# Two gated feed-forward layers: where the norm's factor 1/rms is applied

## The chip, the cores and the metric

The kernel runs on one core of a Trainium2 chip. The metric is the device time of one execution in microseconds, as the median of several runs. The engines are TensorE (PE, with PEld for its weight loads), VectorE (DVE), ScalarE (ACT), GpSimd (POOL) and SyncE (SP), which here only issues DMAs.

## The reference, cut to what matters

256 tokens of width 1024 pass through four layers of a first block (mixer, then feed-forward, each followed by a layer norm) and one layer of a second block: a gated feed-forward layer, a mixer, a second gated feed-forward layer, a last norm. The change concerns the two gated layers:

```python
def rmsnorm(x, g):
    y = x * rsqrt(mean(x * x, -1) + 1e-6)      # one factor for each token
    return y * g                               # one weight for each column

def swiglu(x, w1, w3, w2):                     # w1, w3: 1024 x 2816, w2: 2816 x 1024
    return (silu(x @ w1) * (x @ w3)) @ w2

x = x + 0.5 * swiglu(rmsnorm(x, ffn1_norm), ffn1_w1, ffn1_w3, ffn1_w2)
x = x + hybrid_mixer(rmsnorm(x, mix_norm), ...)
x = x + 0.5 * swiglu(rmsnorm(x, ffn2_norm), ffn2_w1, ffn2_w3, ffn2_w2)
```

Since the factor is the same for all columns of a token, `rmsnorm(x) @ w1` is `((x * g) @ w1)` with each token's sums multiplied by its factor.

## The kernel before, in words

**Weights.** All weights come from memory once, in a fixed order (`STREAM`), in items of up to 128x1024 floats. Each is cast on ScalarE to the rounded four-byte form that TensorE takes at full rate (line 366, the high part), and VectorE subtracts to get the rest (line 367, the low part; most are issued at line 369). Products are three matmuls: high by high, high by low, low by high. `get` (line 408) hands out the next item and first calls `pump`, which issues DMAs up to 8 items ahead and casts and low parts up to 5 items ahead, as far as 6 raw and 7 split buffers allow. The instructions of each engine run in the order in which the code issues them; nothing reorders them.

**Postponed steps.** `then(f, ...)` puts a step on a list, and the next `get` runs the list (`flush`) behind its `pump`. So each step of a chain that is put off in this way lies one weight later than the step before it.

**Rows and boundaries.** Token rows lie in two tiles of 128 tokens, x[0] and x[1]. `boundary` (line 1679) interleaves the end of one layer with the start of the next: the last products of the layer before (`down_tail`), then for each row tile the residual with its norm (`fin`), eight transposes (`to_xT`, line 613, into xT in two halves of 512 columns) and their copies, and between them the first matmuls of the next layer. `ln_rms` and `rms` give the `fin` of the two gated layers; both end in `rms_rows` (line 660): two squares on ScalarE with a sum, one small sum and one scale on VectorE, a power on GpSimd, and two products of 128x512 on VectorE, which multiply the row by the factor and by the weight.

**The front.** `front` (line 525) starts a layer with six weights, numbered 0 to 5 here, in an order that needs the first 128 tokens first. It yields to `boundary` at two stops for the transposes of x[1], then goes through weights 0 to 5 once more with what is left: per weight the last 4 matmuls with the high part and 8 with the low part, then a step of `low_next` (one postponed low part; all postponed ones at weight 3, lines 549 and 550), `flush`, `done` and `pump`. `done` sums the two halves of the weight's bank on VectorE (`front_sum`, line 559).

**The gated layer.** `ffn` (line 1310) has 22 hidden tiles of 128 columns (numbered from 0). The front's six weights are w1 and w3 of tiles 0 to 2; the following weights, numbered on from 6, are w1 and w3 of tile 3, and so on. A tile's two sums (128x256 each) lie in one tile `su`. Behind the second sum, `evac` is put off by a weight: tanh of half the first sum on ScalarE; one weight later `evac_on`: two VectorE steps, (tanh + 1) * a and the product with b, and the cast of the result on ScalarE (line 1327); one weight later the subtraction for its low part. From tile 5 on each tile also has a w2 weight, whose product (`down`, 12 matmuls of 512 columns) takes the hidden tile of five tiles before; the last four hidden tiles go through `down_tail`.

Of the kernel before, what the change touches and what calls it, by code (L numbers as in the profile page):

```python
# [9 lines left out]
F32 = mybir.dt.float32  # L10
F32R = mybir.dt.float32r
I32 = mybir.dt.int32
AF = mybir.ActivationFunctionType
# [5 lines left out]
P = 128  # L19
S = 256  # L20
D = 1024
# [3 lines left out]
RMS_EPS = 1e-6  # L25
# [254 lines left out]
def kernel(ctx, tc, d, out, dbg=None):  # L280
    nc = tc.nc
    ctx.enter_context(tc.manual_schedule())
    nv, ns, ng, nt = nc.vector, nc.scalar, nc.gpsimd, nc.tensor
# [7 lines left out]
    sm = ctx.enter_context(tc.tile_pool(name="sm", bufs=4))  # L291
    accp = ctx.enter_context(tc.tile_pool(name="accp", bufs=1, space=PSUM))
# [4 lines left out]
    def stt(o, a, s, b, op0, op1):  # L297
        nv.scalar_tensor_tensor(out=o, in0=a, scalar=s, in1=b, op0=op0, op1=op1)  # L298

    def tt(o, a, b, op, eng=None):  # L300
        (eng or nv).tensor_tensor(out=o, in0=a, in1=b, op=op)  # L301

    def ts2(o, a, s1, s2, op0, op1):
        nv.tensor_scalar(out=o, in0=a, scalar1=s1, scalar2=s2, op0=op0, op1=op1)  # L304

    def ts1(o, a, s1, op0):
        nv.tensor_scalar(out=o, in0=a, scalar1=s1, scalar2=None, op0=op0)

    def act(o, i, f, **kw):
        ns.activation(out=o, in_=i, func=f, **kw)  # L310

    def mm(o, a, b, start, stop):
        nt.matmul(out=o, lhsT=a, rhs=b, start=start, stop=stop)  # L313

    MUL, ADD, SUB, MAX = ALU.mult, ALU.add, ALU.subtract, ALU.max

    def psb(name="pp"):
        return pp.tile([P, 512], F32, tag="pp", name=name)
# [56 lines left out]
    def then(f, *a):  # L375

        st["then"].append((f, a))
# [30 lines left out]
    def get(name):  # L408
        i = st["i"]
        e = STREAM[i]  # L410
        assert e[1] == name, (i, e, name)
        if not st["pin"]:
            st["base"] = i
        pump(i + 1)
        flush()
        st["i"] += 1
        hl = st["hl"].pop(i)
        if i in WHOLE:
            return hl
        c, kk = _width(e), e[4]  # L420
        return [hl[:, n, :c].rearrange("p (k w) -> p k w", k=kk) for n in range(2)]
# [11 lines left out]
    def ws2(bank, ch, xT, kk, c0=0):  # L433


        h, l = ch
        w = slice(c0, c0 + P)
        for k in range(kk):
            mm(bank, h[:, k, w], xT[:, k], k == 0, False)
            mm(bank[:, :S], l[:, k, w], xT[:, k, 0, :], False, k == kk - 1)  # L440

    def ws2_sum(bank, o):
        nv.tensor_reduce(out=o, in_=bank.rearrange("p (a n) -> p n a", a=2), axis=AX.X, op=ADD)  # L443
# [43 lines left out]
    def acc_new():  # L487
        return [[accp.tile([P, 512], F32, tag=f"a{t}{n}", name=f"a{t}{n}") for n in range(2)]
                for t in range(2)]
# [69 lines left out]
    def front_sum(ps, o):  # L559

        nv.tensor_reduce(out=o.rearrange("p (t n) -> p t n", t=2),
                         in_=ps.rearrange("p (t a n) -> p t n a", t=2, a=2), axis=AX.X, op=ADD)

    def front_banks():

        n = [0]

        def bank():
            n[0] += 1
            if n[0] > 2:  # L570
                return psb("fr")
            tag = f"a0{n[0] - 1}"
            return accp.tile([P, 512], F32, tag=tag, name=tag)
        return bank


    def new_x(t):
        return xp.tile([P, D], F32, tag=f"x{t}", name=f"x{t}")
# [7 lines left out]
    def C(k, a=0, n=None):  # L586
        part, o, w = COFF[k]
        return cs[part][:, o + a:o + (w if n is None else a + n)]

    x = [new_x(t) for t in range(2)]  # L590
# [10 lines left out]
    ident = C("ident")  # L601
# [3 lines left out]
    def rsqrt(o, v, mul, add):  # L605

        n = v.shape[-1]
        e = sm.tile([P, 16], F32, tag="ve", name="ve")
        ts2(e[:, :n], v, mul, add, MUL, ADD)
        tt(o, e[:, :n], mhalf[:, :n], ALU.pow, ng)  # L610
# [22 lines left out]
    halves = [slice(0, 512), slice(512, 1024)]  # L633
# [18 lines left out]
    def residual(x, acc_t, t, c):  # L652
# [4 lines left out]
                yield  # L657
        return z

    def rms_rows(x, g, t):  # L660
        o = new_x(t)
        ss = sm.tile([P, 2], F32, tag="ss", name="ss")
        for n, w in enumerate(halves):
            act(o[:, w], x[:, w], AF.Square, accum_out=ss[:, n:n + 1])
        tt(ss[:, 0:1], ss[:, 0:1], ss[:, 1:2], ADD)
        rs = sm.tile([P, 1], F32, tag="rs", name="rs")
        rsqrt(rs, ss[:, 0:1], 1.0 / D, RMS_EPS)
        for w in halves:
            stt(o[:, w], x[:, w], rs, g[:, w], MUL, MUL)
        return o  # L670
# [636 lines left out]
            yield from down_tail(acc, lambda c: (oT[:, 4 + c], get("mla_w_o")), 4)  # L1307
            fes.close()

    def ffn(seg, xT):  # L1310
        nf = DFF2 // P
        lag = FFN_LAG
        w = [f"ffn{seg}_w{k}_2" for k in (1, 3, 2)]
        tail = TAIL["ffn", seg]
        with tc.tile_pool(name="ffnp", bufs=8) as mp:
            hid = {}

            def evac(j, a, b):
                r = mp.tile([P, S], F32, tag="r", name="r", bufs=2)
                act(r, a, AF.Tanh, scale=0.5)  # L1320
                then(evac_on, j, r, a, b)

            def evac_on(j, r, a, b):
                h = mp.tile([P, 2, S], F32R, tag="h", name="h")
                stt(r, r, 1.0, a, ADD, MUL)
                tt(r, r, b, MUL)
                ns.copy(out=h[:, 0], in_=r)  # L1327
                then(tt, h[:, 1], r, h[:, 0].bitcast(F32), SUB)
                hid[j] = h

            sums = {}

            def done(n, ps):
                if n % 2 == 0:
                    sums[0] = mp.tile([P, 2, S], F32, tag="su", name="su", bufs=3)
                front_sum(ps, sums[0][:, n % 2])
                if n % 2 == 1:
                    then(evac, n // 2, sums[0][:, 0], sums[0][:, 1])

            yield from front([w[k % 2] for k in range(FRONT)], xT, front_banks(), done,  # L1340
                             (4, 5) if seg == 1 else (3, 4))
            acc = acc_new()
            for j in range(FRONT // 2, nf + lag):
                if j < nf:
                    su = mp.tile([P, 2, S], F32, tag="su", name="su", bufs=3)
                    for n in range(2):
                        ps = psb()
                        ws2(ps, get(w[n]), xT, KD)
                        ws2_sum(ps, su[:, n])
                    then(evac, j, su[:, 0], su[:, 1])  # L1350
                c = j - lag
                if c < 0:
                    continue
                if c < nf - tail:
                    ch = get(w[2])
                    for t in range(2):
                        down(acc, t, hid[c], ch, c == 0, False)
            yield from down_tail(acc, lambda j: (hid[nf - tail + j], get(w[2])), tail)
# [320 lines left out]
    def boundary(prev, fin, nxt):  # L1679


        def rest(f):
            while True:
                try:
                    next(f)
                except StopIteration as e:
                    return e.value

        f = fin(0, next(prev))
        next(f)  # L1690
        low_next(1)
        y0 = rest(f)
        xT = new_xT()
        f = fin(1, next(prev))
        next(f)
        to_xT(xT, y0, 0, (0,))
        next(prev)
        to_xT(xT, y0, 0, (1,))
        next(prev)
        next(prev, None)  # L1700
        g = nxt(xT)
        next(g)
        y1 = rest(f)
        to_xT(xT, y1, 1, (0,))
        next(g)
        to_xT(xT, y1, 1, (1,))
        return g
# [6 lines left out]
            return x[t]  # L1714
        return fin

    def ln_rms(i, n, name):
        last = ln(i, n)
        g = rows(name, (0,), tabp, "gC")

        def fin(t, a):
            return rms_rows((yield from last(t, a)), g, t)
        return fin

    def rms(name, c):
        g = rows(name, (0,), gbp, "gB")

        def fin(t, a):
            x[t] = yield from residual(x[t], a, t, c)
            return rms_rows(x[t], g, t)  # L1730
        return fin

    order = [lambda xT: ret(0, xT), lambda xT: mlp(0, xT, hook=early), lru, lambda xT: mlp(1, xT), mla,
# [9 lines left out]
    g = order[0](xT0)  # L1743
    for i in range(7):
        g = boundary(g, ln(i // 2, i % 2), order[i + 1])
# [5 lines left out]
    for t in range(2):  # L1751
        x[t] = new_x(t)
        nc.gpsimd.dma_start(out=x[t], in_=xd[t:S:2, :])
    g = boundary(g, ln_rms(3, 1, "ffn1_norm_2"), lambda xT: ffn(1, xT))
    tap("f3")
    tabs.close()
    g = boundary(g, rms("mix_norm_2", 0.25), lambda xT: mix(xT, bd))
    tap("ffn1")
    g = boundary(g, rms("ffn2_norm_2", 0.5), lambda xT: ffn(2, xT))
    tap("mix")  # L1760
    gf = rows("final_norm_2", (), gbp, "gB")

    for t in range(2):
        a = next(g)
        y = new_x(t)
        ss = sm.tile([P, 2], F32, tag="ss", name="ss")
# [8 lines left out]
        rs = sm.tile([P, 1], F32, tag="rs", name="rs")  # L1775
# [60 lines left out]
```

## Time and profile before

| what | value |
|---|---|
| median of 3 runs | 2014.78 us (2012.68 to 2014.83) |
| the profiled execution's own time | 2014.34 us |
| its span, first to last instruction | 2012.6 us |
| TensorE matmul busy | 1979.8 us, 98% |
| VectorE busy | 1425.1 us, 71% |
| ScalarE busy | 1019.0 us, 51% |
| mean granted clock of TensorE | 0.998 of full speed |

The profile is one execution on the chip. Times in it count from the span's first instruction. In the timeline a row gives the start, the time covered, the engine, the line of the code, the operation, the output and inputs, the shape and the number of merged instructions; in brackets stands the idle time of that engine just ahead of the row and what ended it. The ends of matmuls are modelled, and matmuls are pipelined. The granted clock is given as a share of 2.4 GHz; 0.5 is the level of 1.2 GHz.

### The profile page before, as it was taken

Reading aid. Unit: us, or ns where it says so; the run is one execution under the profiler, and the core shown is the slowest. Engines: PE = TensorE matmul, PEld = TensorE weight load, DVE = VectorE, ACT = ScalarE, POOL = GpSimd, SP = SyncE. Lnnn points to the kernel's source line nnn. Section 1 sums busy time; section 2 is a strip of 40 time slices with the busy share of each in tenths; the row PEclk is TensorE's granted clock in tenths of the full one; section 3 lists DMA queues with packets and bytes.
Section 4 is the critical chain, followed back from the end, with each engine's and each line's share of the span. In section 5 each row is a group of like instructions: output and inputs, shape, how many; then the busy total and the mean of one; then the engine's idle time right before and its main releaser. Section 6 shows DMA issues by size and latency. Waiting matters only on the chain.

```text
span 2012.6 us, 28871 instructions
## 1 busy us (share of the span) xinstructions
PE 1979.8 (98%) x11118; PEld 1708.3 (85%) x11118; DVE 1425.1 (71%) x2057; ACT 1019.0 (51%) x1451; POOL 79.4 (4%) x114
## 2 busy tenths in 40 slices
PE   8999999999999999999999999999999999999998
PEld 6888887887888888888888888888888999998886
DVE  6767876689856688656877875568777755567775
ACT  5444555477555465554444455535444655544443
POOL 0000000000000100000000000000001100000000
PEclk9999999999999999999999999999999999999999
DMA  8654565464755455664655485637655556465652
GB/s 300 183 174 145 192 204 173 145 215 147 238 188 187 135 169 177 201 193 152 220 177 169 136 292 183 195 120 225 190 188 173 154 159 163 137 200 176 210 188 72
DMA packets 102713, 364.53 MB, mean 181 GB/s; under 512 B 11856, under 2 KB 12528, under 8 KB 102577
## 3 DMA queue, kind: packets, MB, share of 16 engines
q1 hardware_dynamic: 97200, 345.09, 53.7%
q0 software_dynamic: 5376, 17.61, 3.5%
q8 instruction: 87, 1.43, 0.3%
q14 instruction: 50, 0.40, 0.1%
HBM read 360.52 MB, written 2.13 MB: 180 GB/s over the span
## 4 chain that ended last, share of the span: by engine, by line
PE 90%; DVE 5%; DMA 1%; ACT 1%; issue 1%; POOL 1%; SPq 0%; POOLq 0%; DVEq 0%; ACTq 0%
PE pp L313 53%; PE a L313 32%; PE fr L313 3%; DVE x L298 1%; DVE hl L301 1%; POOL rs L301 1%; ACT hl L366 1%; DVE bs L640 1%; PE a L621 0%; DMA raw<-in_w_ret_dram 0%; DMA raw<-in_w_mlp_dram 0%; DVE xT L301 0%; PE ao L313 0%; PE a L1578 0%; DMA raw<-in_w_mla_dram 0%
## 5 line engine op out<-in xcount | busy, mean ns | idle before, releaser
L301 DVE TENSOR_TENSOR hl<-raw,hl 128x1024 fp32r<-128x1024 f32 (+3 forms) x659 | 774.5, 1198 | 217.6 <-ACT hl L366 215.7
L366 ACT CAST hl<-raw 128x1024 fp32r<-128x1024 f32 (+3 forms) x659 | 661.8, 1032 | 343.9 <-PE a L313 169.8
L313 PE MATMUL pp<-xT,hl 128*128 128x512 f32 (+1 forms) x4688 | 784.2, 324 | 0.6 <-ACT hl L366 0.3
L313 PEld LDWEIGHTS pp<-xT,hl 128*128 128x128 f32 x4688 | 685.8, 189 | 86.7 <-issue 3.1
L313 PE MATMUL a<-hl,h 128*128 128x512 f32 x2064 | 502.1, 394 | 0.0
L313 PEld LDWEIGHTS a<-hl,h 128*128 128x128 f32 x2064 | 381.4, 190 | 80.9
L313 PE MATMUL pp<-hl,xT 128*128 128x512 f32 (+2 forms) x1200 | 270.8, 381 | 2.7 <-ACT hl L366 1.6
L313 PEld LDWEIGHTS pp<-hl,xT 128*128 128x128 f32 x1200 | 219.6, 189 | 41.5 <-DVE xT L301 2.0
L443 DVE TENSOR_REDUCE su<-pp 128x256 f32<-128x512 f32 x180 | 124.0, 689 | 165.1 <-PE pp L313 161.6
L310 ACT ACTIVATE su<-su 128x512 f32<-128x512 f32 x128 | 81.0, 633 | 132.0 <-DVE su L443 122.2
L301 POOL TENSOR_TENSOR rs<-ve,mhalf 128x1 f32<-128x1 f32 (+2 forms) x48 | 41.9, 875 | 1682.5 <-DVE ve L304 1682.5
L313 PE MATMUL a<-hl,yT 128*128 128x512 f32 x432 | 104.0, 397 | 0.0
L313 PEld LDWEIGHTS a<-hl,yT 128*128 128x128 f32 x432 | 80.7, 188 | 18.8 <-issue 0.5
L313 PE MATMUL fr<-xT,hl 128*128 128x256 f32 x672 | 88.7, 285 | 0.0
L313 PEld LDWEIGHTS fr<-xT,hl 128*128 128x128 f32 x672 | 83.8, 193 | 0.0
L1327 ACT CAST h<-r 128x256 fp32r<-128x256 f32 x44 | 17.9, 407 | 127.1 <-DVE r L301 127.1
L313 PE MATMUL a<-xT,hl 128*128 128x256 f32 x336 | 46.6, 289 | 3.9 <-DVE xT L301 3.9
L313 PEld LDWEIGHTS a<-xT,hl 128*128 128x128 f32 x336 | 42.9, 195 | 7.5 <-DVE xT L301 7.5
L298 DVE SCALAR_TENSOR_TENSOR x<-x,a 128x512 f32<-128x512 f32 x32 | 21.8, 683 | 32.9 <-PE a L313 32.9
L301 DVE TENSOR_TENSOR h<-su,h 128x512 fp32r<-128x512 f32 x64 | 43.8, 685 | 0.9 <-ACT h L785 0.9
L785 ACT CAST h<-su 128x512 fp32r<-128x512 f32 x64 | 39.7, 620 | 2.0
L322 ACT CAST xT<-a 128x512 fp32r<-128x512 f32 x22 | 12.8, 586 | 42.6 <-PE a L621 42.6
(356 smaller groups left out, 1343.7 us busy)
## 6 DMA issues: line engine op xcount, KB each, us to landing
raw<-in_w_mlp_dram SPq DMA_DIRECT2D x256, 512.0 KB, 4.0
raw<-in_w_ffn_dram SPq DMA_DIRECT2D x132, 512.0 KB, 4.1
raw<-in_w_ret_dram SPq DMA_DIRECT2D x128, 512.0 KB, 4.4
raw<-in_w_mix_dram SPq DMA_DIRECT2D x68, 512.0 KB, 4.2
raw<-in_w_lru_dram SPq DMA_DIRECT2D x30, 512.0 KB, 4.6
raw<-in_w_mla_dram SPq DMA_DIRECT2D x12, 512.0 KB, 4.5
raw<-in_w_mix_dram SPq DMA_DIRECT2D x16, 384.0 KB, 4.3
gB<-in_ln_g_dram POOLq DMA_DIRECT2D x8, 512.0 KB, 4.5
```

The source lines that it names most:

```text
L298: nv.scalar_tensor_tensor(out=o, in0=a, scalar=s, in1=b, op0=op0, op1=op1)
L301: (eng or nv).tensor_tensor(out=o, in0=a, in1=b, op=op)
L310: ns.activation(out=o, in_=i, func=f, **kw)
L313: nt.matmul(out=o, lhsT=a, rhs=b, start=start, stop=stop)
L322: ns.copy(out=h, in_=src)
L366: ns.copy(out=hl[:, 0, :c], in_=t[:, :c])
L443: nv.tensor_reduce(out=o, in_=bank.rearrange("p (a n) -> p n a", a=2), axis=AX.X, op=ADD)
L640: nv.bn_stats(out=bs[:, n], in_=z[:, w])
L785: ns.copy(out=h[:, :, 0], in_=r)
L1327: ns.copy(out=h[:, 0], in_=r)
```

## The change

For the two gated layers, `rms_rows` is replaced by `gain_rows`: the row tile is multiplied by the norm's weight alone and goes on to the transposes. The squares, the sum and the power for the factor are issued later, in `done` of the front's weight 0. At `done` of weight 4, `factors` builds two diagonal matrices with the factors of the 256 tokens, multiplies a matrix of ones by them on TensorE, so that every partition holds the factor of each token along its columns, and copies the result to `fac`. Each hidden tile's pair of sums is multiplied by `fac` (one VectorE product of 128x512) ahead of its tanh. The first two tiles' `evac` are put on the list at weight 4 and the third's at weight 5 (before: at weights 1, 3 and 5). The mixer between the two layers keeps `rms_rows`.

```diff
+    def gain_rows(x, g, t, rms):
+
+        o = new_x(t)
+        for w in halves:
+            tt(o[:, w], x[:, w], g[:, w], MUL)
+        rms[t] = sm.tile([P, 1], F32, tag="rs", name="rms")
+
+        def factor():
+            sq = accp.tile([P, 512], F32, tag="a11", name="sq")
+            ss = sm.tile([P, 2], F32, tag="ss", name="ss")
+            for n, w in enumerate(halves):
+                act(sq, x[:, w], AF.Square, accum_out=ss[:, n:n + 1])
+            tt(ss[:, 0:1], ss[:, 0:1], ss[:, 1:2], ADD)
+            rsqrt(rms[t], ss[:, 0:1], 1.0 / D, RMS_EPS)
+        rms[t, "f"] = factor
+        return o
...
-    def ffn(seg, xT):
+    def ffn(seg, xT, rms):
...
-            def evac(j, a, b):
-                r = mp.tile([P, S], F32, tag="r", name="r", bufs=2)
+            fac = mp.tile([P, S], F32, name="fac", bufs=1)
+
+            def factors():
+
+                one = mp.tile([P, P], F32, name="one", bufs=1)
+                nv.memset(one, 1.0)
+                ps = psb()
+                for t in range(2):
+                    dg = mp.tile([P, P], F32, name=f"dg{t}", bufs=1)
+                    ts1(dg, ident, rms[t], MUL)
+                    mm(ps[:, t * P:(t + 1) * P], one, dg, True, True)
+                ns.copy(out=fac, in_=ps[:, :S])
+
+            def evac(j, su):
+                tt(su, su, fac[:, None, :].to_broadcast([P, 2, S]), MUL)
+                a, b = su[:, 0], su[:, 1]
+                r = mp.tile([P, S], F32, tag="r", name="r", bufs=4)
                 act(r, a, AF.Tanh, scale=0.5)
                 then(evac_on, j, r, a, b)
...
             def done(n, ps):
                 if n % 2 == 0:
-                    sums[0] = mp.tile([P, 2, S], F32, tag="su", name="su", bufs=3)
-                front_sum(ps, sums[0][:, n % 2])
-                if n % 2 == 1:
-                    then(evac, n // 2, sums[0][:, 0], sums[0][:, 1])
+                    sums[n // 2] = mp.tile([P, 2, S], F32, tag="su", name="su", bufs=3)
+                front_sum(ps, sums[n // 2][:, n % 2])
+                if n == 0:
+                    for t in range(2):
+                        rms[t, "f"]()
+                elif n == 4:
+                    factors()
+                    for j in range(2):
+                        then(evac, j, sums[j])
+                elif n == 5:
+                    then(evac, 2, sums[2])
...
-                    then(evac, j, su[:, 0], su[:, 1])
+                    then(evac, j, su)
...
-            return rms_rows((yield from last(t, a)), g, t)
+            return gain_rows((yield from last(t, a)), g, t, rms)
...
-            return rms_rows(x[t], g, t)
+            return rms_rows(x[t], g, t) if later is None else gain_rows(x[t], g, t, later)
```

## Rows read from the trace of the kernel before

**Rows 1.** The page, busy time and share of the span by engine.
```profile
PE 1979.8 (98%) x11118; PEld 1708.3 (85%) x11118; DVE 1425.1 (71%) x2057; ACT 1019.0 (51%) x1451; POOL 79.4 (4%) x114
```

**Rows 2.** Timeline of the boundary into the first gated layer.
```profile
1331.49 0.63 PE L621 MATMUL trp<-cs,x 128*128 128x128 f32 x4 [1.02 <-DVE x L298]
...
1334.52 1.22 PE L313 MATMUL a<-xT,hl 128*128 128x256 f32 x8 [0.55 <-DVE xT L301]
...
1339.37 0.75 DVE L298 SCALAR_TENSOR_TENSOR x<-x,rs,bB 128x512 f32<-128x512 f32 x1
1340.15 0.63 ACT L310 ACTIVATE x<-x 128x512 f32<-128x512 f32 x1 [0.73 <-DVE x L298]
...
1342.79 0.66 PE L621 MATMUL a<-cs,x 128*128 128x128 f32 x4 [2.73 <-DVE x L298]
...
1344.84 2.07 PE L313 MATMUL a<-xT,hl 128*128 128x256 f32 x8 [0.34 <-DVE xT L301]
```

**Rows 3.** Windows after that wait: busy time by engine, granted clock, DMA.
```profile
1344.00:1346.00 2.00, 1.66 (x9) 1.28 (x8) 1.54 (x3) 0.65 (x2) 0.00 (x0) 0.52 0.43 145
1346.00:1348.00 2.00, 2.00 (x13) 2.00 (x12) 2.00 (x2) 0.00 (x0) 0.00 (x0) 0.63 0.04 2
```

**Rows 4.** Timeline of the boundary into the second gated layer, TensorE.
```profile
1822.22 0.60 PE L621 MATMUL a<-cs,x 128*128 128x128 f32 x4
...
1824.22 1.22 PE L313 MATMUL a<-xT,hl 128*128 128x256 f32 x8
```

**Rows 5.** Timeline of the fronts, first layer (one row), then second layer.
```profile
1354.69 4.62 DVE L301 TENSOR_TENSOR hl<-raw,hl 128x1024 fp32r<-128x1024 f32 x4
...
1828.84 0.69 DVE L561 TENSOR_REDUCE su<-a 128x256 f32<-128x512 f32 x1 [0.35 <-PE a L313]
1828.88 1.05 ACT L366 CAST hl<-raw 128x1024 fp32r<-128x1024 f32 x1 [4.53 <-PE a L313]
1829.45 1.22 DVE L301 TENSOR_TENSOR hl<-raw,hl 128x1024 fp32r<-128x1024 f32 x1
...
1830.08 5.92 PE L313 MATMUL fr<-xT,hl 128*128 128x256 f32 x48
...
1832.92 3.48 DVE L301 TENSOR_TENSOR hl<-raw,hl 128x1024 fp32r<-128x1024 f32 x3
```

**Rows 6.** Timeline of one tile of the first gated layer, VectorE and ScalarE.
```profile
1392.48 0.68 DVE L443 TENSOR_REDUCE su<-pp 128x256 f32<-128x512 f32 x1
1392.60 0.41 ACT L1327 CAST h<-r 128x256 fp32r<-128x256 f32 x1 [3.08 <-DVE r L301]
...
1393.98 1.23 DVE L301 TENSOR_TENSOR hl<-raw,hl 128x1024 fp32r<-128x1024 f32 x1 [0.82 <-ACT hl L366]
...
1395.13 0.42 DVE L301 TENSOR_TENSOR h<-r,h 128x256 fp32r<-128x256 f32 x1
...
1396.06 2.35 DVE L301 TENSOR_TENSOR hl<-raw,hl 128x1024 fp32r<-128x1024 f32 x2
1398.33 0.41 DVE L298 SCALAR_TENSOR_TENSOR r<-r,su 128x256 f32<-128x256 f32 x1
...
1399.12 0.68 DVE L443 TENSOR_REDUCE su<-pp 128x256 f32<-128x512 f32 x1
```

**Rows 7.** Window over nine tiles of the first gated layer, later on.
```profile
1408.73:1484.51 75.78, 75.78 (x400) 64.64 (x399) 53.08 (x74) 34.07 (x46) 0.00 (x0) 1.00 0.61 189
```

**Rows 8.** Groups by line and shape, VectorE: count, busy us, mean ns.
```profile
L301 DVE TENSOR_TENSOR q<-ra,cosr 128x512 f32<-128x512 f32 x8 | 5.5, 683 | 0.0
...
L304 DVE TENSOR_SCALAR ve<-mv 128x1 f32<-128x1 f32 x32 | 4.9, 154 | 1.1
...
L307 DVE TENSOR_SCALAR pe<-pe,sums 128x256 f32<-128x256 f32 x16 | 4.9, 350 | 0.3
```

**Rows 9.** Timeline, TensorE behind the last hidden weight of each layer.
```profile
1509.33 15.50 PE L313 MATMUL a<-hl,h 128*128 128x512 f32 x66
...
1986.94 16.89 PE L313 MATMUL a<-hl,h 128*128 128x512 f32 x72
```

More of the change, by code (lines that the diff above doesn't have):

```diff
@@ L1715, in ln, with ln_gain @@
         return fin
-    def ln_rms(i, n, name):
+    def ln_gain(i, n, name, rms):
         last = ln(i, n)
@@ L1721, in fin, with rms @@
         def fin(t, a):
-            return rms_rows((yield from last(t, a)), g, t)
+            return gain_rows((yield from last(t, a)), g, t, rms)
         return fin
-    def rms(name, c):
+    def rms(name, c, later=None):
         g = rows(name, (0,), gbp, "gB")
@@ L1753 @@
         nc.gpsimd.dma_start(out=x[t], in_=xd[t:S:2, :])
-    g = boundary(g, ln_rms(3, 1, "ffn1_norm_2"), lambda xT: ffn(1, xT))
+    later = {}
+    g = boundary(g, ln_gain(3, 1, "ffn1_norm_2", later), lambda xT: ffn(1, xT, later))
     tap("f3")
@@ L1758 @@
     tap("ffn1")
-    g = boundary(g, rms("ffn2_norm_2", 0.5), lambda xT: ffn(2, xT))
+    later2 = {}
+    g = boundary(g, rms("ffn2_norm_2", 0.5, later2), lambda xT: ffn(2, xT, later2))
     tap("mix")
```

## The prediction

> **What bounds the kernel now.** I read the page first: TensorE is busy 98% of the span [rows 1], so only two kinds of stretch can move the time, those where TensorE stands still and those where its clock is low. The timeline of the two places where a gated layer begins comes next, since the change takes work off the chain there. At the first layer (from 1330 us) TensorE waits for the second half of the normed rows: the last residual row block is ready at 1339.37 + 0.75 = 1340.12, the squares, the sum, the power on GpSimd and the product follow, and the transposes start at 1342.79 after 2.73 us of idle time; the first half had cost 1.02 and 0.55 us [rows 2]. The windows right after show the granted clock at 0.52 and 0.63, so a part of them ran at the 1.2 GHz level [rows 3]. At the second layer there is no such wait: transposes at 1822.22 and matmuls at 1824.22 follow without a stop [rows 4]. So the norm's chain is worth something at one of the two layers only.
>
> The stretch behind that, the front of six weights, I read on VectorE. It is behind TensorE there: in the second layer TensorE ends the front at 1830.08 + 5.92 = 1836.0, and VectorE only then ends three low parts of later weights (1832.92 + 3.48); in the first layer it is four (4.62 us) [rows 5]. Then I read how VectorE gets out of that backlog [rows 6], and its share once it is out [rows 7].
>
> **What goes.** At the first layer the transposes of the second half need only the gain product of its first 512 columns, 0.69 us after 1340.12, where they now come 2.67 us after it: 1.94 us. The first half gains between 0 and the 1.57 us of its two waits; four casts of weights stand ahead of its transpose copies on ScalarE, which the two squares no longer hold up, but which wait for buffers that TensorE frees, so I take 0.8. The front's second part, at 1344.84 now, starts at 1342.1. The clock, after a wait of some 0.8 us instead of 2.73, should stay up. That is worth more than 0.85 (the first eight matmuls take 2.07 here and 1.22 in the second layer [rows 2, 4]) and less than (1 - 0.52) x 1.66 + (1 - 0.63) x 2.00 = 1.54, the busy time of the two windows that the clock took [rows 3]; I take 1.15. The scaled products of before (0.70) become plain products (0.69): nothing. At the second layer I take 0.
>
> **What is moved.** Four squares (0.63 each [rows 2]) go to ScalarE behind the first front weight. ScalarE is idle there, 4.53 us before its cast at 1828.88 [rows 5], so they cost nothing; uncovered they would be 2.5 us and more. Four small VectorE operations of 0.15 us [rows 8] do cost VectorE some 0.75 us per layer with the steps between them, behind the sum of weight 0. No DMA is moved; two powers on GpSimd come later and are not waited for.
>
> **What is added, first term: the wait for the factor.** The two products of ones by the diagonal stand in TensorE's queue between the matmuls of front weight 4 and those of weight 5. They wait for two diagonals, which VectorE makes behind the sum of weight 4. VectorE's own order up to there, from the restart R of the front's second part: sum of weight 0 at R + 4.62 (1824.22 to 1828.84), 0.61 to its end, 0.75 small operations, two low parts and two sums 3.47 (1829.45 to 1832.92), three low parts 3.42 (four: 4.56), sum 0.60, the low part of weight 10 1.14, sum of weight 4 0.68 [rows 4, 5]. The ones and two diagonals have no row of their own: a scalar product takes 0.15 us at one column and 0.35 at 256 [rows 8], so together between 0.4 and 1.0; I take 0.65, nearer to the small end as they have 128 columns. Sum: R + 15.9 in the second layer, R + 17.1 in the first. TensorE has ended weight 4 at R + 11.78 - 1.48 = R + 10.3 (weight 5 is a quarter of the last 48 matmuls, 5.92). So TensorE waits 5.6 us in the second layer and 6.8 in the first; queued behind are weight 5 and all later weights. The product itself is two matmuls of 128 columns in four-byte floats, as the transposes are, four of which take 0.60 [rows 4]: 0.3.
>
> **Second term: the loop between VectorE and ScalarE.** Each hidden tile now has a product of 128x512 ahead of its tanh; the same shape with a broadcast operand takes 0.683 us [rows 8]. What matters is its place. ScalarE runs tanh of a tile, then the cast of the next weight, and VectorE's next instruction is the low part that needs this cast. Before, tanh needs only a sum that is there, so the cast is early. Now tanh waits for the product. The trace has this very hand-over: a ScalarE operation on 256 columns at 1392.60, the cast behind it, the low part at 1393.98, 1.38 later with VectorE idle for 0.82 [rows 6]. So a tile gets 0.68 + 0.03 + 1.38 = 2.09 longer on VectorE where VectorE is the one behind. There its period is 1399.12 - 1392.48 = 6.64 us per tile now, which shrinks the backlog by 1.78 per tile, as TensorE needs 75.78 / 9 = 8.42 [rows 6, 7]. With the change it is 8.73: the backlog no longer shrinks, it grows by 0.31 per tile.
>
> How far VectorE is by then, from T, when the factor product starts: copy of the factor done at T + 0.9; then three tiles have to be multiplied at once and their steps crowd. The steps are those of rows 6: a low part 1.14 (two from 1396.06 to 1398.33), a tile's two steps 0.79 (1398.33 to 1399.12), or 0.87 to the end of the second, a subtraction 0.33 (0.93 from 1395.13 to 1396.06, less a sum), a hand-over 0.03 + 1.38. The low part of weight 11 starts at T + 3.8; weight 12 comes 4.84 later (a low part 1.14, four tile steps 1.60, a product 0.68, hand-over 1.41), weight 13 another 4.08 later (low part, two subtractions 0.66, two steps 0.87, hand-over), then six weights at 3.56 and 3.42 by turns (low part with subtraction, product and hand-over; low part with two steps and hand-over), 20.9; and 1.47 to the second sum of tile 6: T + 35.1. Then 15 tiles of 8.73 to the same sum of tile 21: T + 166.1. By TensorE alone this sum could start at T + 154.5 (0.3 for the product, 1.5 for weight 5, 1.15 for the clock, 54 weights of 8.42 / 3), so it comes 11.6 us late. Until there TensorE hardly feels it, as weights are split five ahead. It feels it at the end: the last tile still needs its low part, product, tanh, two steps, cast and subtraction, 6.73 us in the first layer (with a low part of the next layer's weight between) and 4.65 in the second, and TensorE reaches this tile 33 matmuls after the last hidden weight, 33 x 0.2346 = 7.74 [rows 9].
>
> The last tile's first matmul (it can start 0.47 before the subtraction ends, as the third one reads it): first layer 1342.1 + 17.1 + 166.1 + 6.73 - 0.47 = 1531.5, now 1509.33 + 7.74 = 1517.1: 14.4 later. Second layer 1824.2 + 15.9 + 166.1 + 4.65 - 0.47 = 2010.4, now 1986.94 + 7.74 = 1994.7: 15.7 later. These contain the waits for the factor and the gain at the first layer. Most of it is one long wait for the last tiles in each layer, about 10 and 8.5 us by the sums of the first rival below, longer than the 2.73 us after which the clock fell, so I add 1.15 for each, 2.3 (between 0 and 4). Sum 32.4.
>
> The sum goes on the profiled execution's own 2014.34 us (span 2012.6), 0.44 below the median of the runs: **2046.7 us**.
>
> **Rivals.** *Only the waits for the factor* (2025.7 us). VectorE keeps up with its extra product, and what is left is 6.8 + 0.3 + 1.15 (clock) less 2.74 and 1.15 at the first layer, that is 4.3, and 5.6 + 0.3 + 1.15 = 7.1 at the second: 11.4. For it: over nine tiles VectorE is busy 53.08 of 75.78 us, 70%, and nine products of 0.68 make 78% [rows 7]. Against it: the period is made of hand-overs, not of busy time, and rows 6 show VectorE idle in each while it is behind. The Trainium skill, Perfetto Trace Analysis, section Identifying the Most-Contended Engine, says that for the vector engine occupancy is what shows the bottleneck and how near to its limit it is. By that rule 78% is no bound, and the time is this rival's; the trace doesn't agree where VectorE is behind, as it is the one that the others wait for in rows 6 and still idle for 0.82 of 6.64 us.
>
> *Faster* (2011 us). The factor is there when TensorE comes to it: VectorE, which starts earlier and has the tile steps of the front put off, has no backlog at weight 4. Then the wait is the sum of weight 4, the ones and the diagonals, 1.3 us, or none; the first layer gives 2.74 + 1.15 = 3.9 and the products take 0.6. It decides at a wait of 1.6 us per layer. Against it are the three and four low parts in VectorE's order ahead of that sum [rows 5]; nothing in the trace takes them out.
>
> *More than forecast* (2058 us): the hand-overs cost 0.3 more per tile, 15 x 0.3 x 2 = 9, and the clock falls for longer after the waits, 2.
>
> **Chances.** Forecast 0.72, only the waits 0.16, more 0.06, faster 0.04, no difference 0.02. The forecast's own range is 2036 to 2055 (0.15 per tile either way is 4.5, the crowded start 2 per layer, the clock 2). Leaving out no more than 2 in 10 on both sides, and with the bounds of the unknown operations, the range is 2023 to 2058. A difference below 0.2%, 4 us, couldn't be told from none: faster 0.04, same 0.02, slower 0.94.
>
> **What would show it.** In the profile after: transposes of the first layer's second half without the 2.73 us; a TensorE wait for a diagonal of 5 to 7 us in each layer, behind front weight 4; VectorE without waits for TensorE's sums in the layers' middle, the sums 5 to 11 us behind the matmuls, and a period near 8.7; TensorE waiting for the last hidden tiles, 8 us or so, with a granted clock below 1 right after. The forecast is wrong if VectorE waits for TensorE again by the tenth tile (then about 2026), or if the wait for the diagonal is under 1.6 us (then faster).

## The result and the profile after

The changed kernel takes 2056.7 us (median of four runs, 2054.33 to 2058.24), the kernel before 2013.73 beside it (four runs): ratio 1.0212, 95% interval 1.02 to 1.0223. It is slower by 43 us; 32.4 were forecast. The profiled execution took 2057.59 us with a span of 2055.8.

Page of the kernel after, busy time, share of the span and instructions by engine (compare [rows 1]):

```profile
PE 1994.6 (97%) x11126; PEld 1716.4 (83%) x11126; DVE 1453.8 (71%) x2107; ACT 1019.2 (50%) x1453; POOL 80.6 (4%) x114
```

By this page little has happened: no share has moved by more than two points. TensorE's waits tell more. Kernel after, waits of TensorE over the span (the view gives what it waited for, us in total, how often, longest):

```profile
PE pp L313 <- DVE dg L307: 11.3, 2, 6.2
PE a L313 <- ACT h L1358: 8.7, 2, 5.3
PE a L621 <- DVE x L298: 4.7, 1, 4.7
...
PE a L313 <- ACT hl L366: 3.9, 4, 1.4
PE a L313 <- DVE hl L301: 3.0, 4, 0.8
```

The diagonals (dg), the last hidden tiles (h, and the low parts just ahead of them), and a wait of 4.7 us for normed rows at a place that the change doesn't touch.

Kernel after, timeline of TensorE in the first layer: the front's start, the wait for the diagonals, the layer's end, the entry into the mixer. The bracket at a row's end is the idle time before it, and what ended it:

```profile
1333.64 1.22 PE L313 MATMUL a<-xT,hl 128*128 128x256 f32 x8 [0.81 <-DVE xT L301]
...
1339.90 0.66 PE L621 MATMUL a<-cs,x 128*128 128x128 f32 x4 [0.72 <-DVE x L301]
...
1341.96 1.22 PE L313 MATMUL a<-xT,hl 128*128 128x256 f32 x8 [0.48 <-DVE xT L301]
...
1358.51 1.20 PE L313 MATMUL pp<-dg,one 128*128 128x128 f32 x4 [6.21 <-DVE dg L307]
1359.36 2.71 PE L313 MATMUL fr<-xT,hl 128*128 128x256 f32 x12
...
1524.52 0.50 PE L313 MATMUL a<-hl,h 128*128 128x512 f32 x1 [1.44 <-ACT hl L366]
1525.78 1.22 PE L313 MATMUL a<-hl,h 128*128 128x512 f32 x2 [0.76 <-DVE hl L301]
1532.32 9.52 PE L313 MATMUL a<-hl,h 128*128 128x512 f32 x33 [5.32 <-ACT h L1358]
...
1554.67 1.11 PE L621 MATMUL a<-cs,x 128*128 128x128 f32 x4 [4.68 <-DVE x L298]
```

Of the 2.73 us wait of the boundary [rows 2] 0.72 is left: from the first half's matmuls to the second half's it is now 8.32 us (1333.64 to 1341.96), where it was 10.32 (1334.52 to 1344.84). The waits below, from the diagonals on, are new or longer. Before, TensorE ran the products of the last hidden tiles in one piece [rows 9] and waited 0.40 us at the mixer; kernel before, the same place:

```profile
1533.39 0.66 PE L621 MATMUL a<-cs,x 128*128 128x128 f32 x4 [0.40 <-DVE x L298]
```

Kernel after, timeline of VectorE, one tile in the layer's last third (compare [rows 6]):

```profile
1505.47 0.68 DVE L443 TENSOR_REDUCE su<-pp 128x256 f32<-128x512 f32 x1
1506.98 1.23 DVE L301 TENSOR_TENSOR hl<-raw,hl 128x1024 fp32r<-128x1024 f32 x1 [0.82 <-ACT hl L366]
...
1510.19 0.68 DVE L301 TENSOR_TENSOR su<-su,fac 128x512 f32<-128x512 f32 x1
1512.30 1.23 DVE L301 TENSOR_TENSOR hl<-raw,hl 128x1024 fp32r<-128x1024 f32 x1 [1.42 <-ACT hl L366]
...
1514.23 0.69 DVE L443 TENSOR_REDUCE su<-pp 128x256 f32<-128x512 f32 x1
```

From sum to sum it takes 8.76 us. VectorE waits only for ScalarE's casts, once 0.82 us as before and, after each product, another 1.42. Its waits from 1365 to 1532 us are these alone:

```profile
DVE hl L301 <- ACT hl L366: 42.4, 39, 1.5
```

It doesn't wait for TensorE, so it is the one behind.

**Where the 43 us are.** Profiled executions of the same instructions reach the first gated layer at scattered times (the eight changed kernels of this study between 1330.7 and 1333.6 us), so I compare two stretches, each from the first front matmuls on the first half's rows: of the first layer to that of the second ("first layer and mixer"), and from there to the end of the span. For the second these rows are, in the kernel before:

```profile
1817.34 1.21 PE L313 MATMUL a<-xT,hl 128*128 128x256 f32 x8 [0.37 <-DVE xT L301]
```

and in the kernel after:

```profile
1840.86 1.22 PE L313 MATMUL a<-xT,hl 128*128 128x256 f32 x8 [0.38 <-DVE xT L301]
...
1863.14 1.19 PE L313 MATMUL pp<-dg,one 128*128 128x128 f32 x4 [5.05 <-DVE dg L307]
...
2034.83 12.10 PE L313 MATMUL a<-hl,h 128*128 128x512 f32 x39 [3.34 <-ACT h L1358]
```

| kernel | first layer and mixer, us | second layer to the end, us | time, median, us | ratio to before, 95% interval |
|---|---|---|---|---|
| before | 482.8 | 195.3 | 2013.7 to 2014.1 | 1 |
| after | 507.2 | 214.9 | 2056.7 | 1.0212 (1.02 to 1.0223) |
| pool at its old size | 502.3 | 214.7 | 2052.3 | 1.0189 (1.0175 to 1.0203) |
| tanh later | 493.4 | 202.4 | 2030.4 | 1.0082 (1.0068 to 1.0096) |
| diagonals earlier | 505.5 | 212.7 | 2052.0 | 1.0186 (1.0172 to 1.02) |
| change in first layer only | 507.3 | 195.4 | 2037.6 | 1.0117 (1.0103 to 1.013) |
| all three edits | 481.6 | 195.9 | 2012.8 | 0.9994 (0.9985 to 1.0002) |
| all three, first layer only | 481.2 | 195.3 | 2011.1 | 0.9987 (0.9978 to 0.9996) |
| product on GpSimd | 513.3 | 219.5 | 2067.8 | 1.0272 (1.0257 to 1.0288) |

So 24.4 us are lost in the first stretch and 19.7 in the second; 0.9 us are won ahead of both, by the transposes of the first half.

### The profile page after: what moved, and what is told of

Read it like the earlier page. It is cut to its first block, busy times and chain, and to the rows that moved or that the text cites. A ratio compares the mean times of both kernels' runs of the same rounds, so it can differ in the third digit from the quotient of the medians.

```text
span 2055.8 us, 28905 instructions
## 1 busy us (share of the span) xinstructions
PE 1994.6 (97%) x11126; PEld 1716.4 (83%) x11126; DVE 1453.8 (71%) x2107; ACT 1019.2 (50%) x1453; POOL 80.6 (4%) x114
## 3 DMA queue, kind: packets, MB, share of 16 engines
q8 instruction: 87, 1.43, 0.3%
HBM read 360.52 MB, written 2.13 MB: 176 GB/s over the span
## 4 chain that ended last, share of the span: by engine, by line
PE 85%; DVE 8%; ACT 3%; issue 2%; DMA 2%; POOL 1%; SPq 0%; POOLq 0%; ACTq 0%; DVEq 0%
PE pp L313 50%; PE a L313 30%; PE fr L313 3%; DVE hl L301 2%; ACT hl L366 2%; DVE x L298 2%; POOL rs L301 1%; DVE bs L640 1%; PE a L621 0%; DMA raw<-in_w_mlp_dram 0%; DMA raw<-in_w_ret_dram 0%; DMA raw<-in_w_ffn_dram 0%; DVE xT L301 0%; PE ao L313 0%; PE a L1616 0%
## 5 line engine op out<-in xcount | busy, mean ns | idle before, releaser
L313 PE MATMUL a<-hl,h 128*128 128x512 f32 x2064 | 510.6, 398 | 15.8 <-ACT h L1358 8.7
L310 ACT ACTIVATE r<-su 128x256 f32<-128x256 f32 x44 | 18.4, 418 | 112.2 <-DVE su L301 112.2
```

## The experiments

The theory after the first look: (1) a tile's hand-over from VectorE's product to ScalarE's tanh and cast and back to VectorE's low part makes VectorE's period longer than TensorE's, and the layers end late by that; (2) TensorE's wait for the diagonals is mostly hidden by (1); (3) the wait at the mixer comes from memory: the layer's pool had grown. Rivals: VectorE has too much work; each wait of TensorE is paid in full; the mixer's loads are merely late.

**The layer's pool at its old size.** By the sizes of its buffers the layer's pool takes 24 KB per partition before and 28.5 KB after (factor 1, ones and diagonals 1.5, two more r buffers 2). The mixer's first pool takes the place of the layer's and is 24 KB long; the pool with the mixer's tables lies behind it, so it now began inside the layer's old place. That its start lay on h buffers is read from the wait shown below, which ends with TensorE's products of h.

```
-  one = mp.tile([P, P], F32, name="one", bufs=1)
+  one = mp.tile([P, S], F32, tag="r", name="one", bufs=3)[:, :P]
...
+  dgs = mp.tile([P, S], F32, tag="r", name="dg", bufs=3)
-  dg = mp.tile([P, P], F32, name=f"dg{t}", bufs=1)
+  dg = dgs[:, t * P:(t + 1) * P]
...
-  r = mp.tile([P, S], F32, tag="r", name="r", bufs=4)
+  r = mp.tile([P, S], F32, tag="r", name="r", bufs=3)
-  h = mp.tile([P, 2, S], F32R, tag="h", name="h")
+  h = mp.tile([P, 2, S], F32R, tag="h", name="h", bufs=7)
```

> The changed kernel with the layer's pool back at its old 24 KB per partition: the ones and the two diagonals live in two of the r buffers, r has three buffers instead of four, h seven instead of eight. No instruction is added, removed or moved. Theory (memory): in the changed kernel the pool had grown to 28.5 KB and reached into the first buffers of the mixer's pool behind it, so the loads of the mixer's tables waited 3.94 us for the layer's last matmuls, and TensorE then 4.68 us for the normed rows. With the old size neither wait is there: TensorE's second half of the transposes at the mixer's boundary waits 0.4 us as before, the 4.3 us and the 2.25 us that the clock cost behind it go, and the time is 2050 us (2056.7 - 6.6). Rival (lateness): the loads are late because VectorE and ScalarE reach that boundary late in the changed order; then the wait of 4.7 us and the 2056.7 us stay.

2052.3 us. Its five times (2050.26 to 2053.28) lie below all four of the kernel after (2054.33 to 2058.24), though the intervals of the two ratios overlap a little; the traces show where the difference is. Timeline at the entry into the mixer, GpSimd's load of the table and VectorE's first use of it, kernel after:

```profile
1544.74 0.59 POOL L1426 DMA_DIRECT2D ax<-in_consts_dram  x1 [3.94 <-PE a L313]
...
1548.57 0.83 DVE L301 TENSOR_TENSOR rt<-ax,gq 128x256 f32<-128x256 f32 x3 [3.56 <-DMA gq<-in_q_norm_dram]
```

and with the pool at its old size, with TensorE's transposes that follow:

```profile
1539.39 0.59 POOL L1427 DMA_DIRECT2D ax<-in_consts_dram  x1
...
1543.70 0.83 DVE L301 TENSOR_TENSOR rt<-ax,gq 128x256 f32<-128x256 f32 x3 [0.19 <-DMA gq<-in_q_norm_dram]
...
1549.88 0.66 PE L621 MATMUL a<-cs,x 128*128 128x128 f32 x4 [1.43 <-DVE x L298]
```

The load no longer waits for TensorE's last matmuls of the layer, VectorE's products and the residual row block queued behind them come earlier, TensorE waits 1.43 instead of 4.68, and its four transposes take 0.66 instead of 1.11. Of the 24.4 us lost in the first stretch 4.9 come back, in the second stretch next to nothing (0.2). I had expected 6.6: a wait of 1.3 to 1.5 us, and not 0.4, stays in every version with the old size (in the one with all three edits VectorE there waits 0.83 us for the second small table); why that is so stays open. The memory theory holds; lateness as the main cause is out.

**The tanh one weight later than the product.**

```
   def evac(j, su):
       tt(su, su, fac[:, None, :].to_broadcast([P, 2, S]), MUL)
+      then(evac_tanh, j, su)
+
+  def evac_tanh(j, su):
       a, b = su[:, 0], su[:, 1]
...
-  su = mp.tile([P, 2, S], F32, tag="su", name="su", bufs=3)
+  su = mp.tile([P, 2, S], F32, tag="su", name="su", bufs=4)
```

> The changed kernel with the tanh one weight later than the product: the product is issued at one weight's call, the tanh at the next, the rest at the one after; four buffers of sums instead of three, seven of h instead of eight, so that the pool keeps its 28.5 KB. Same instructions. Theory (hand-over): in the changed kernel a tile takes 8.76 us, because VectorE's product, the tanh behind it on ScalarE and the low part behind ScalarE's cast wait for each other once per tile (1.38 us); TensorE needs 8.42. With the tanh later ScalarE no longer waits for the product in front of its casts, a tile takes VectorE some 7.4 us, the waits at each layer's end (5.3 and 3.3 us, and those of 0.5 to 1.4 us before them) go, and what is left of each layer is the wait for the diagonals: about 10 us less in each layer and 2 us of clock behind each, 2032 us. Rival (work): VectorE's added 0.68 us per tile is itself what is too much; then the waits at the ends stay and the time is 2054 to 2059 us.

2030.4 us, 26 us back with not one instruction less. Timeline of VectorE, the same part of a tile:

```profile
1482.76 0.69 DVE L301 TENSOR_TENSOR su<-su,fac 128x512 f32<-128x512 f32 x1
1483.37 1.22 DVE L301 TENSOR_TENSOR hl<-raw,hl 128x1024 fp32r<-128x1024 f32 x1
1485.65 0.69 DVE L443 TENSOR_REDUCE su<-pp 128x256 f32<-128x512 f32 x1 [1.07 <-PE pp L313]
```

The low part follows the product at once, and VectorE waits for TensorE's sums: TensorE is the bound again. Of the new waits only that for the diagonals is left in this layer (6.2 us), and 4.2 at the mixer. The fourth buffer of sums can't be what did it: in the kernel after VectorE, which writes the sums, waited for nothing but casts. The hand-over theory holds; the work theory (2054 to 2059) falls.

**The product on GpSimd**, which asks the same from the other side: VectorE gets less work, the hand-over gets longer.

```
-  tt(su, su, fac[:, None, :].to_broadcast([P, 2, S]), MUL)
+  tt(su, su, fac[:, None, :].to_broadcast([P, 2, S]), MUL, ng)
```

> The changed kernel with the product of the sums and the factor on GpSimd instead of VectorE, at the same place in the order. VectorE has 0.68 us less to do per tile, GpSimd some 24 products per layer of a size that no row has shown on it so far (the smallest products it has, 128x1, show 0.5 to 1 us). Theory (hand-over): VectorE's low part still waits for the cast behind the tanh behind the product, so the work that VectorE loses comes back as waiting; a tile takes no less than 8.7 us, the waits at the layers' ends stay, and the time is 2055 us, or more by 24 times what the product takes longer on GpSimd, up to 2100 us. Rival (work: VectorE's 0.68 us per tile are what is too much): the period falls to 8.42 us, the waits at the ends go, 2030 to 2038 us.

2067.8 us, slower still. Timeline of one tile with the product on GpSimd, GpSimd, ScalarE and VectorE:

```profile
1475.84 1.22 DVE L301 TENSOR_TENSOR hl<-raw,hl 128x1024 fp32r<-128x1024 f32 x1
1476.07 2.13 POOL L301 TENSOR_TENSOR su<-su,fac 128x512 f32<-128x512 f32 x1 [7.18 <-DVE su L443]
...
1478.24 0.42 ACT L310 ACTIVATE r<-su 128x256 f32<-128x256 f32 x1 [3.55 <-POOL su L301]
1478.56 1.03 ACT L366 CAST hl<-raw 128x1024 fp32r<-128x1024 f32 x1
...
1479.63 1.23 DVE L301 TENSOR_TENSOR hl<-raw,hl 128x1024 fp32r<-128x1024 f32 x1 [2.57 <-ACT hl L366]
```

Product, tanh, cast, low part: one chain, and VectorE stands idle for 2.57 us at its end. But the run doesn't test the hand-over alone. The product starts while a low part of VectorE runs, and takes 2.13 us; in the same run's first tiles, where it starts before the low part, it takes 1.29, and the low part takes 1.69 instead of 1.23:

```profile
1371.77 1.29 POOL L301 TENSOR_TENSOR su<-su,fac 128x512 f32<-128x512 f32 x1 [7.84 <-DVE su L443]
1372.45 1.69 DVE L301 TENSOR_TENSOR hl<-raw,hl 128x1024 fp32r<-128x1024 f32 x1 [0.83 <-ACT hl L366]
```

So some 0.84 us (2.13 - 1.29) of each later tile go with the two engines' running at the same time. By this estimate a tile would take about 8.5 us without them, less than the 8.7 expected. That the work VectorE loses comes back as waiting, 2055 us or more, is therefore not shown by this run; the later tanh is what decides between the two theories.

Three windows put the versions side by side: nine tiles of the kernel after, nine with the tanh later, eight with the product on GpSimd. Columns: window, length, then busy time (instructions) of PE, PEld, DVE, ACT, POOL, then the granted clock, DMA share and GB/s.

```profile
1426.58:1505.47 78.89, 78.85 (x412) 66.64 (x411) 58.33 (x82) 33.04 (x45) 0.00 (x0) 1.00 0.62 180
```

```profile
1410.18:1485.65 75.47, 75.47 (x397) 64.41 (x396) 59.17 (x81) 33.07 (x45) 0.00 (x0) 1.00 0.63 189
```

```profile
1397.72:1472.26 74.54, 74.54 (x394) 63.62 (x393) 47.06 (x66) 29.37 (x40) 17.11 (x8) 1.00 0.56 170
```

Per tile 8.77, 8.39 and 9.32 us; VectorE is busy 74%, 78% and 63%. The version in which VectorE is busiest is the fast one, the one in which it has least to do the slowest. PE shows as busy throughout in all three, at 0.19 us per matmul (78.89 / 412, 75.47 / 397, 74.54 / 394): in the first and third it goes ahead on weights that are already split, while VectorE falls further behind. TensorE pays late in the layer, when that lead is used up, first by running at VectorE's period and then by the waits at the end.

**The diagonals two weights earlier**, behind the sum of the third front weight; their products with the ones stay behind the fifth.

```
+  elif n == 2:
+      sums["f"] = factors()          # ones and diagonals only
   elif n == 4:
-      factors()
+      spread(*sums.pop("f"))         # products with the ones, copy
```

> The changed kernel with the two diagonals made right behind the sum of the third weight of the front instead of the fifth; their products with the ones and the copy stay behind the fifth. Same instructions. TensorE's wait for the diagonals (6.2 us in the first layer, 5.05 in the second) should go in any case. Theory (the loop of VectorE and ScalarE sets the layer's end): VectorE reaches the first product only some 1.5 to 2 us earlier, its low parts are no earlier, and TensorE waits for these later in the layer instead; each layer ends about 2 us earlier, 2053 us (2051 to 2055). Rival (each wait of TensorE is paid in full): both waits and the clock behind them go, 6.2 + 1.2 and 5.05 + 1.2 us, and the time is 2043 us.

2052.0 us. Timeline of TensorE in the first layer:

```profile
1349.21 0.61 PE L313 MATMUL pp<-dg,one 128*128 128x128 f32 x4
1349.57 1.68 PE L313 MATMUL fr<-xT,hl 128*128 128x256 f32 x12
1352.23 10.04 PE L313 MATMUL pp<-xT,hl 128*128 128x512 f32 x55 [0.98 <-ACT fac L1349]
...
1527.74 9.67 PE L313 MATMUL a<-hl,h 128*128 128x512 f32 x33 [5.41 <-ACT h L1362]
```

The 6.21 us wait is gone, and with it the low clock: the same 16 matmuls took 1.20 and 2.71 behind the wait and 0.61 and 1.68 here. Yet the wait at the layer's end is as long as ever (5.41), and the stretches are only 1.7 and 2.2 us shorter. Where the rest went is seen in the middle of the first layer; TensorE's w2 products of two tiles in turn, diagonals earlier:

```profile
1412.74 2.96 PE L313 MATMUL a<-hl,h 128*128 128x512 f32 x12
1421.51 2.96 PE L313 MATMUL a<-hl,h 128*128 128x512 f32 x12
```

A tile takes TensorE 8.77 us here already, VectorE's period, with no long wait in it; in the kernel after the same products still came every 8.39 us on average, from 1378 to 1487. At the first w2 product TensorE was some 6 us ahead of the kernel after (both counted from the first front matmuls), at the last hidden tiles 1.6. So what was taken from TensorE's path was given back in the middle of the layer, at VectorE's pace, and the waits at the end stayed. That waits of TensorE are paid in full (2043) falls.

**The change in the first layer alone** (the second layer, `ffn_old`, and its boundary as in the kernel before):

```
-  g = boundary(g, rms("ffn2_norm_2", 0.5, later2), lambda xT: ffn(2, xT, later2))
+  g = boundary(g, rms("ffn2_norm_2", 0.5), lambda xT: ffn_old(2, xT))
```

> The change in the first of the two layers alone; the second layer is that of the kernel before (its rows are normed at the boundary, no factor). Theory (the layers' costs add up): what the trace of the changed kernel lies behind at the end of the mixer stays, 15.25 at the layer's last wait, 1.7 of clock, 4.3 at the mixer's boundary, 2.25 of clock, 23.5 us in all, and the second layer adds nothing: 2037 us. The prediction's own sum for the first layer, 14.4 and 1.15, would give 2029 us. Rival (what is late is taken up again): lateness of the first layer is absorbed in the mixer, 2014 to 2025 us.

2037.6 us, 23.5 more than before; the other 19.1 (2056.7 - 2037.6) come with the second layer. The two layers' losses add up, and nothing of the first is taken up in the mixer.

**All three edits together**, in both layers and in the first alone; to keep 24 KB with four buffers of sums, ones and diagonals take two of three r buffers and h has six.

> The changed kernel with the three edits together, in both layers: the tanh one weight after the product, the diagonals behind the sum of the third weight, and the pool at 24 KB (ones and diagonals in r buffers, three of r, four of sums, six of h). Each alone measured 2030.4, 2052.0 and 2052.3 against the changed kernel's 2056.7. Theory (three causes that add up once the loop no longer sets the layer's end): the later tanh leaves 2030.4; from this go the two waits for the diagonals, which are now TensorE's alone to pay (6.2 and 5.05 us, of which 1.0 to 1.7 us stay as waits for the copy and the low parts), 1.2 us of clock behind each, and 4.4 us at the mixer's boundary: 2030.4 - 9 - 2.4 - 4.4 = 2014.6 us (2011 to 2018), no different from the kernel before. Rival (VectorE's backlog): with TensorE 7 us earlier in each layer VectorE's low parts come too late again, the waits return at tiles 3 to 8 or at the layers' ends, and the time is 2020 to 2027 us.

2012.8 us, ratio 0.9994 (0.9985 to 1.0002): no difference from the kernel before. Behind the front of the first layer TensorE waits 0.95 us for the copy of the factor, and at no other place until the mixer, so VectorE's backlog as a rival falls. First stretch 481.6, second 195.9.

> The three edits together in the first layer alone; the second layer is that of the kernel before. What the change takes away at the first layer's boundary is then all that is left of it: TensorE's second half of the front began 2.9 us earlier in the trace of the changed kernel than before, without the drop of the clock. Theory (the boundary's gain is real): 2014.1 - 2.9 - 1.2 of clock + 1.7 of waits for the copy and the low parts + 1 at the mixer's boundary = 2012.7 us (2010 to 2014). Rival (the gain is given back, VectorE's backlog): 2014 us or more, and the last hidden tile's first matmul in the first layer not before 1517.1.

2011.1 us, ratio 0.9987 (0.9978 to 0.9996): faster by 0.13% at the middle, which is less than the 0.2% that the prediction counted as a difference. The last hidden tile's first matmul in the first layer follows the first front matmuls after 179.9 us, before after 182.6 (1334.52 to 1509.33 + 7.74, [rows 2, 9]). So the boundary's gain is real, but small: 2.7 us here and some 0.9 ahead of the first front matmuls, less 1.1 at the mixer (a wait of 1.49 instead of 0.40). The medians differ by 2.7. The prediction's sum for this gain, the waits of [rows 2] and the clock behind them, was 3.9, which the new wait for the copy (0.70) and the products with the ones lessen.

## Why the prediction was right, and where it was short

Direction and mechanism were right, and so were all places that the forecast named; one place, the entry into the mixer, it didn't name. The time lies in the range (2023 to 2058), 1.7 us above the likeliest case's own (2036 to 2055). That it stays inside the range is partly luck: the upper end came from longer hand-overs, which were not there, and 6.6 of the missing 10.8 us lie at a place where the prediction had put nothing. Point by point:

- **What goes.** The second half's matmuls at 1342.1 forecast, 1341.96 measured; no drop of the clock there (the first eight take 1.22). Right, though by its own numbers the 1.94 should read 1.98 (2.67 - 0.69). The first half gained 0.95 us where 0.8 was taken: from the start of the last 89 products of the layer before it, first in the kernel before, then in the kernel after, it is 24.81 us to the front's first matmuls (1334.52) and 23.86 (1333.64):

```profile
1309.71 20.76 PE L313 MATMUL a<-hl,h 128*128 128x512 f32 x89
```

```profile
1309.78 20.76 PE L313 MATMUL a<-hl,h 128*128 128x512 f32 x89
```

- **What is moved.** The four squares lay in ScalarE's idle time; the small VectorE steps took 0.5 us per layer, where 0.75 was costed. Right.
- **The wait for the factor.** 6.8 and 5.6 us forecast, 6.2 and 5.05 measured; the diagonals, counted with the ones as 0.65, took 0.5. Right. The products with the ones were mis-sized: 0.3 us forecast, 0.61 measured at full clock and 1.20 behind the wait, so the first tile's product with the factor came 1.63 us after their start, where 0.9 was taken for the copy:

```profile
1360.14 1.29 DVE L301 TENSOR_TENSOR su<-su,fac 128x512 f32<-128x512 f32 x2 [1.59 <-ACT fac L1345]
```

  That the wait for the factor mostly runs beside the lateness of VectorE, so that the layer's end counts and not the wait, is what the earlier diagonals showed.
- **The loop.** Period 8.73 forecast, 8.76 measured. The last tile's second sum was forecast 166.1 us after the start of the products with the ones, and came 167.5 after it in both layers (from 1358.51 and 1863.14):

```profile
1525.97 0.68 DVE L443 TENSOR_REDUCE su<-pp 128x256 f32<-128x512 f32 x1
...
2030.56 0.68 DVE L443 TENSOR_REDUCE su<-pp 128x256 f32<-128x512 f32 x1
```

  From there to the last tile's first matmul 6.26 and 4.18 us were forecast, 6.35 and 4.27 measured. This is the step that the later tanh was made to break, and it bore it out. The layers' ends came at +15.25 and +16.6 against 14.4 and 15.7: the wait for the factor was 0.55 us shorter, the way to the last sum 1.4 longer.
- **The clock after the waits: mis-sized.** I took 1.15 us for each layer's end. At full clock 33 and 39 of these matmuls take 7.74 and 9.15 (0.2346 each [rows 9]); they took 9.52 and 12.10: 1.8 and 2.95. The granted clock of the kernel after in three windows, behind the diagonals, and behind the last tile of the first and of the second layer:

```profile
1360.00:1362.00 2.00, 2.00 (x12) 2.00 (x12) 1.29 (x2) 1.06 (x4) 0.00 (x0) 0.58 0.45 180
...
1532.00:1536.00 4.00, 3.69 (x9) 2.97 (x10) 2.25 (x3) 2.16 (x3) 0.00 (x0) 0.53 0.49 131
...
2034.00:2038.00 4.00, 3.17 (x8) 2.50 (x9) 2.15 (x4) 1.13 (x3) 0.00 (x0) 0.50 0.00 0
```

  The price of 1.15 came from one wait of 2.73 us. At the layers' ends TensorE had also run one or two matmuls at a time between several waits, and the level of 1.2 GHz (granted clock 0.50 to 0.53 over 4 us) cost more. That was 2.4 us too little. Why it cost 2.95 behind the shorter last wait and 1.8 behind the longer, no run shows.
- **Not foreseen: the memory.** "No DMA is moved" looked at the order of the instructions only. The change's new buffers moved the pool's end past the start of the next pool; the first load into that pool waited for the layer's last matmuls, and TensorE waited 4.3 us more, with about 2.25 of clock behind it (from those transposes to the first of `bq` 27.80 us, before 25.52). The old size brought 4.9 of these 6.6 back.

Sum of the shortfall: 1.75 at the layers' ends, 2.4 of clock and 6.6 at the mixer are 10.8, and 32.4 + 10.8 = 43.2, the difference of the two profiled spans (2055.8 - 2012.6).

Of the rivals, "only the waits for the factor" (2025.7) is nearly what the later tanh made of the kernel (2030.4, with the memory's part in it): it described a kernel with another order. The rule of the Trainium skill that speaks for it (Perfetto Trace Analysis, section Identifying the Most-Contended Engine: the vector engine's occupancy tells how near it is to its limit) isn't borne out by the windows above: the chain through VectorE held the layer up with VectorE at 74% and 63%, and didn't at 78%. The sum of "more than forecast" (2058) came nearest to the time, though not by its reasons: the period was not 0.3 us longer.

## What to carry to other kernels

An operation put ahead of another engine's work can cost what the chain through both queues costs, not its own duration: here 0.68 us of work made 2.1 us per tile where VectorE was behind (6.64 before [rows 6], 8.76 after), and moving the consumer one step later in the order took 26 of 43 us back. Follow one whole period through all engines' queues, and compare it with the bound engine's, before reading occupancy. Where a change adds buffers, look up whether a pool behind it now overlaps, and what is loaded there first.

## What was not expected of the hardware

A product of 128x512 in four-byte floats took GpSimd 1.27 to 1.30 us, where VectorE takes 0.69, but 2.11 to 2.15 when it started while a low part of VectorE was running; the low part then kept its 1.22. Where the product started first, the low part took 1.69. So the one that started second was the slower; no run varies this by itself. The product of the ones and a diagonal, one matmul of 128 columns in the code, stands in the trace as two records each (x4 for two), 0.61 us for all at full clock and 1.20 at the low level. The transposes, by which the prediction had sized it, stand as one record each.
